# Gates of the dense stage computed for two keys at a time, and looser order edges on the row steps

## The chip, the core and the metric

One NeuronCore of a Trainium2 chip runs the whole program in one launch. The metric is device time in microseconds (us). TensorE (PE) does matmuls and weight loads (PEld), VectorE (DVE) and ScalarE (ACT) do elementwise work, GpSimd (POOL) issues the indirect row fetches, and SyncE (SP) issues most plain DMAs. Each engine takes its instructions strictly in the order of its own queue.

## What is computed

A residual block on 1024 tokens of width 1024: a mixer (gated delta rule and a linear recurrence), cross attention into 256 memory tokens, and a retrieval layer that picks 128 of 16384 single-neuron experts for each token. The change touches the last of these:

```python
idx = e1 * PEER_NKEYS + e2                # 8 heads x 16 experts for each token
gate = jax.nn.softmax(best, axis=-1)
act = jax.nn.gelu(jnp.einsum('phkd,pd->phk', u_tab[ib], tb)) * gb
out = jnp.einsum('phk,phkd->pd', act, v_tab[ib])
```

All of it is float32.

## The kernel before

The retrieval layer is done in two ways. For tokens 256 to 767 (TD = 512) it is **dense**: all 16384 experts are run through the PE in 128 chunks of 128 experts ("keys" here), with a gate matrix that is zero for experts not chosen. For the other 512 tokens, in four blocks of 128, it is done by **rows**: for each of the 128 chosen experts of a token POOL fetches one row of u (and later of v) for all 128 tokens of the block by an indirect DMA of 512 KB, and DVE does one 128x1024 operation on it, a "row step". That makes 4 blocks x 2 phases x 128 = 1024 row steps.

*The front part* (up to about 1790 us) holds the mixer, the attention, the choice of experts and the gate matrix, interleaved as streams by a function `together` (L1180 on), which chooses the next piece by times that the builder estimates for itself. Row steps are mixed in by `Paced.tick`: each time the estimated PE time since the last one passes `pe.pace`, one `step()` is traced (L1142). In the front part it is also held back while the estimated DVE time is far ahead or the next row isn't estimated to have landed (`late_row`, L1139).

*The dense part* (`dense`, L1020 to L1103) goes through the keys with `hidden(j)` and `out(j)`. `hidden(j)` splits u and v of a key into a high and a low part (ACT makes `uh`, `vh`, DVE `ul`, `vl`), does 24 matmuls of 512 columns into the one PSUM bank `dh`, then ACT applies GELU into `dg`, DVE multiplies by the gates `G[:, :, j % EC]` (a read with a step of 8 elements), ACT casts to `dah`, and DVE makes the low part `dal`. `out(j)` does 24 matmuls for each key in six banks `po`, and, at odd keys, the fourth token block for two keys in a single bank `po3` (12 more matmuls, in two lots of 6), which DVE adds into `acc`. So the PE has 24 + 18 matmuls for an even key and 24 + 30 for an odd one. The order traced is hidden(0), and then for each j: hidden(j+1), out(j). In the dense part the pace is 2250 ns of estimated PE time for a step (`PACE_D`).

A row goes through six buffers (NROW): five fetches are kept ahead, and POOL can issue the next fetch only when the DVE step that used its buffer is over. The framework's scheduler orders each engine's queue after tracing. It takes work by the traced order among what it believes ready, so that an instruction may be put ahead of an earlier one that it believes is still waiting. `tc.keep_in_program_order` gives a row step an edge behind the DVE instruction that was traced directly before it; the scheduler may put it later, but not earlier.

Of the kernel before, what the change touches and what calls it, by code (L numbers as in the profile page):

```python
# [8 lines left out]
F = mybir.dt.float32  # L9
BF = mybir.dt.bfloat16  # L10
FR = mybir.dt.float32r
I32 = mybir.dt.int32
U32 = mybir.dt.uint32
AF = mybir.ActivationFunctionType
OP = mybir.AluOpType
# [3 lines left out]
S = 1024  # L19
# [4 lines left out]
TD = 2 * T  # L24
EC = 8
# [11 lines left out]
HOP, SLACK, WAIT = 100.0, 8000.0, 1000.0  # L37
SHARE = (6.0, 1.0, 6.0, 1.0)
L_NORM, L_STEP, L_CONV, L_SOFT, L_GATE = 14000.0, 2500.0, 4000.0, 6000.0, 1500.0
PACES = (2800.0, 2800.0, 2800.0, 3500.0)  # L40
PACE_G, PACE_D = 3500.0, 2250.0
FIRST = 0
EARLY = T
UNITS = ((0, 1), (128, 1), (256, 2), (512, 2), (768, 2))
# [5 lines left out]
def block_kernel(ctx: ExitStack, tc: tile.TileContext, a):  # L50
# [17 lines left out]
    def moved(n):  # L68
        dma[0] = max(dma[0], pe.at) + n / 360.0
        return dma[0] + 2000.0  # L70

    class Engine:

        def __init__(self, engine, fixed, rate):
            self.engine, self.fixed, self.rate = engine, fixed, rate
            self.at = self.total = self.end = 0.0

        def __getattr__(self, op):
            call = getattr(self.engine, op)

            def f(*args, **kw):
                r = call(*args, **kw)  # L82
                aps = [x for x in list(args) + list(kw.values()) if isinstance(x, bass.AP)]
                if op == "dma_start":
                    moved(prod(args[0].shape) * 4)
                else:
                    self.spend(aps)
                return r
            return f

# [32 lines left out]
    pe = Paced()  # L123
    sp = Engine(nc.sync, 0.0, 0.0)
    act, dve = Engine(nc.scalar, 200.0, 0.72), Engine(nc.vector, 68.0, 1.04)
# [119 lines left out]
    def c8(t):  # L245
        return t.rearrange("p (c m) -> p c m", c=8)
# [67 lines left out]
    def mm3(out, l, r, start, stop):  # L314
        pe.matmul(out, l[0], r[0], start=start, stop=False)
        pe.matmul(out, l[0], r[1], start=False, stop=False)
        pe.matmul(out, l[1], r[0], start=False, stop=stop)
# [692 lines left out]
    def u_raw(p, j):  # L1010
        raw = p.tile([128, D], F, name="ur", bufs=2)
        sp.dma_start(raw, a["ut"][j])
        return raw

    def v_raw(p, j):
        raw = p.tile([128, D], F, name="vr", bufs=2)
        sp.dma_start(raw, a["v"][j * 128:(j + 1) * 128, :])
        return raw

    def dense(p1, p, ps, hT, raws):  # L1020
        hhi, hlo = hT
        NT = TD // 128
        res = [[ps.tile([128, 512], F, name=f"po{t}{d}") for d in range(2)] for t in range(NT - 1)]
        acc = p.tile([128, D], F, name="acc", bufs=1)
        row3 = D0 + TD - 128
        sp.dma_start(acc, x2d[row3:row3 + 128, :])

        def split(raw, name, bufs):
            hi = p1.tile([128, D], FR, name=name + "h", bufs=bufs)
            lo = p1.tile([128, D], FR, name=name + "l", bufs=bufs)  # L1030
            act.copy(hi, raw)
            dve.tensor_sub(lo, raw, hi.bitcast(F))
            return hi, lo

        G = [None]
        A, V = {}, {}

        def hidden(j):
            if j % EC == 0:
                G[0] = p.tile([128, TD, EC], F, name="G", bufs=2)  # L1040
                sp.dma_start(G[0], gd[j // EC])
            u, v = raws.pop(0) if raws else (u_raw(p1, j), v_raw(p1, j))
            uh, ul = [c8(t) for t in split(u, "u", 2)]
            V[j] = split(v, "v", 3)
            h = ps.tile([128, TD], F, name="dh")
            for c in range(8):
                mm3(h, (uh[:, c, :], ul[:, c, :]), (hhi[:, c, :], hlo[:, c, :]), c == 0, c == 7)
            g = p.tile([128, TD], F, name="dg", bufs=2)
            act.activation(g, h, AF.Gelu_apprx_tanh)
            dve.tensor_mul(g, g, G[0][:, :, j % EC])  # L1050
            ah = p.tile([128, TD], FR, name="dah", bufs=3)
            al = p.tile([128, TD], FR, name="dal", bufs=3)
            act.copy(ah, g)
            dve.tensor_sub(al, g, ah.bitcast(F))
            A[j] = (ah, al)

        xs = []

        def add_res(t):
            x = xs[0][:, t, :]  # L1060
            for d in range(2):
                ds = slice(d * 512, (d + 1) * 512)
                dve.tensor_add(x[:, ds], x[:, ds], res[t][d])
            finish(x, D0 + t * 128, xs[0][:, NT - 1, :])

        def out(j):
            def part(o, i, t, d, start, stop):
                ts, ds = slice(t * 128, (t + 1) * 128), slice(d * 512, (d + 1) * 512)
                mm3(o, [x[:, ts] for x in A[i]], [x[:, ds] for x in V[i]], start, stop)

            def last(d):
                o = ps.tile([128, 512], F, name="po3")
                for i in (j - 1, j):
                    part(o, i, NT - 1, d, i < j, i == j)
                ds = slice(d * 512, (d + 1) * 512)
                dve.tensor_add(acc[:, ds], acc[:, ds], o)

            if j == 124:
                xs.append(p.tile([128, TD, EC], F, name="G", bufs=2).rearrange("p (t d) k -> p t (d k)", t=4))
                sp.dma_start(xs[0][:, 0:NT - 1, :],  # L1080
                             x2d[D0:row3, :].rearrange("(t p) m -> p t m", p=128))
            if j % 2:
                last(0)
            for t in range(NT - 1):
                for d in range(2):
                    part(res[t][d], j, t, d, j == 0, j == 127)
                if j == 127:
                    add_res(t)
            if j % 2:
                last(1)  # L1090
                for i in (j - 1, j):
                    A.pop(i), V.pop(i)

        hidden(0)
        for j in range(128):
            if j + 1 < 128:
                hidden(j + 1)
            for _ in range(LATE):
                next(late[0], None)
            out(j)  # L1100
        finish(acc, row3, xs[0][:, NT - 1, :])
# [1 line left out]

    todo, fetched = [], []
    blocks = {}

    def add_block(row, rs, idx, gt):
# [29 lines left out]
    def late_row():  # L1139
        return bool(fetched) and fetched[0][4] > max(dve.at, pe.at) + WAIT  # L1140

    def step():  # L1142
        while todo and len(fetched) < NROW - 1:
            fetch()
        if not fetched:
            return False
        row, ph, k, t, _ = fetched.pop(0)
        B = blocks[row]
        if ph == "u":
            if k == 0:  # L1150
                dve.scalar_tensor_tensor(B["h"], B["h"], B["rs"], B["w"], op0=OP.mult, op1=OP.mult)
                B["hd"] = gat.tile([128, 128], F, name="hdot", bufs=1)
            tc.keep_in_program_order(
                dve.scalar_tensor_tensor(t, t, 1.0, B["h"], op0=OP.mult, op1=OP.mult,
                                         accum_out=B["hd"][:, k:k + 1]))
            if k == 120:
                B["x"] = row_of(NROW + 1)
                sp.dma_start(B["x"], x2d[row:row + 128, :])
            if k == 127:
                B["a"] = gat.tile([128, 128], F, name="ga", bufs=1)  # L1160
                act.activation(B["a"], B["hd"], AF.Gelu_apprx_tanh)
                dve.tensor_mul(B["a"], B["a"], B["gt"].rearrange("p h k -> p (h k)"))
        else:
            tc.keep_in_program_order(
                dve.scalar_tensor_tensor(B["x"], t, B["a"][:, k:k + 1], B["x"], op0=OP.mult, op1=OP.add))
            if k == 127:
                finish(B["x"], row, t)
        return True
# [74 lines left out]
    def attended():  # L1243
        yield from memory(att, KT, VM)
        first.rank = FIRST
        for t0, nb in UNITS:
            while t0 not in done:
                yield None
            yield from attend(att, t0, nb, KT, VM)
        while D0 + TD - T not in begun:  # L1250
            yield None
        front.close()
        d1 = ctx.enter_context(tc.tile_pool(name="duv", bufs=1))
        dn.append(d1)
        raws.extend((u_raw(d1, j), v_raw(d1, j)) for j in range(2))

    dn, hT, raws, begun = [], [], [], set()
    wp = front.enter_context(tc.tile_pool(name="wp", bufs=1))
    att = front.enter_context(tc.tile_pool(name="att", bufs=1))
    KT = att.tile([128, 8, MEM], F, name="KT")  # L1260
# [3 lines left out]
    fps.close()  # L1264
    with tc.tile_pool(name="dn", bufs=1, side="right") as d2, \
            tc.tile_pool(name="dps", bufs=1, space=bass.MemoryType.PSUM) as dps:
        pe.pace, pe.real = PACE_D, False
        dense(dn[0], d2, dps, hT, raws)
    while step():
        pass  # L1270

# [63 lines left out]
```

## Time and profile before

| quantity | us |
|---|---|
| median of 3 runs | 3276.9 (3274.99 to 3279.72) |
| time of the profiled execution | 3275.43 |
| span of the profiled execution, first to last instruction | 3273.7 |
| PE busy in the span | 2987.4 (91%) |
| DVE busy | 2737.6 (84%) |
| ACT busy | 1277.8 (39%) |
| POOL busy | 1431.4 (44%) |

The busy shares are means over two unlike parts, so they are read by stretch below: the front part up to 1790 us, the dense part after it, and in the front part the stretches with and without row steps.

### The profile page before, as it was taken

To read this page: it belongs to the slowest core of one execution; us is meant where nothing else is said; L and a number is where in the kernel's file an instruction comes from. 1 tells how busy PE (TensorE), PEld (TensorE's weight loads), DVE (VectorE), ACT (ScalarE), POOL (GpSimd) and SP (SyncE) were. 2 spreads that over 40 slices of the span, in tenths; PEclk is the share of its full clock that TensorE was granted. 3 is DMA by queue.
4 is the path that set the end of the run, shared out by engine and by line. 5 is a ranking of instruction groups with operands and counts; after the bars stand their busy time and mean duration, and the time that the engine had idled before them with its cause. 6 is when DMAs were issued, how large, how long until landed. Compare 5 with 4: busy or idle time off the path is not lost.

```text
span 3273.7 us, 46519 instructions
## 1 busy us (share of the span) xinstructions
PE 2987.4 (91%) x16212; PEld 2559.6 (78%) x16212; DVE 2737.6 (84%) x5999; ACT 1277.8 (39%) x2694; POOL 1431.4 (44%) x1046
## 2 busy tenths in 40 slices
PE   6999997699999989898857899999999999999998
PEld 6888887678988878887746677888888878888886
DVE  7634776877787898898999798888999989899998
ACT  6843363236322642376357332222222222222222
POOL 0000233334433344243345375556666655566663
PEclk9999998899999999998968899999999999999999
DMA  5346788688888769888888799999999899999995
GB/s 170 110 143 208 248 281 308 232 285 284 308 292 291 251 223 332 301 281 302 303 289 273 267 329 334 333 340 330 344 333 328 319 334 333 330 341 327 339 331 198
DMA packets 321547, 941.66 MB, mean 288 GB/s; under 512 B 28912, under 2 KB 108832, under 8 KB 319264
## 3 DMA queue, kind: packets, MB, share of 16 engines
q0 software_dynamic: 148048, 538.04, 46.8%
q1 hardware_dynamic: 107216, 367.08, 30.9%
q10 hardware_dynamic: 66048, 33.56, 3.7%
q8 instruction: 128, 2.10, 0.3%
q14 instruction: 107, 0.88, 0.1%
HBM read 894.53 MB, written 44.04 MB: 287 GB/s over the span
## 4 chain that ended last, share of the span: by engine, by line
PE 61%; DVE 20%; DMA 9%; ACT 5%; issue 3%; POOL 1%; SPq 0%; ACTq 0%; DVEq 0%; POOLq 0%
PE dh L106 21%; PE po L106 20%; PE pj L106 15%; DVE rb L82 6%; DMA rb<-in_u,idx 4%; PE gd L106 3%; DVE oh L82 3%; DMA gd<-stage 2%; DMA w<-in_pwq 1%; PE tp L111 1%; PE sc L106 1%; DVE cy L82 1%; ACT ohg L82 1%; DVE i L82 1%; ACT L82 1%
## 5 line engine op out<-in xcount | busy, mean ns | idle before, releaser
L1134 POOL DMA_INDIRECT rb<-in_u,idx x512 | 677.4, 1323 | 1111.9 <-DVE rb L82 497.0
L1134 POOL DMA_INDIRECT rb<-in_v,idx x512 | 745.0, 1455 | 690.3 <-DVE rb L82 478.7
L82 DVE SCALAR_TENSOR_TENSOR rb<-rb 128x1024 f32<-128x1024 f32 x512 | 613.1, 1218 | 90.2 <-DMA rb<-in_u,idx 90.2
L82 DVE SCALAR_TENSOR_TENSOR rb<-rb,ga 128x1024 f32<-128x1024 f32 x512 | 655.0, 1279 | 11.2 <-DMA rb<-in_v,idx 4.9
L106 PE MATMUL pj<-hT,w 128*128 128x256 f32 (+1 forms) x2880 | 590.6, 358 | 16.2 <-DMA w<-in_pwq 11.8
L106 PEld LDWEIGHTS pj<-hT,w 128*128 128x128 f32 x2880 | 491.8, 195 | 73.5 <-DMA w<-in_pwq 13.1
L106 PE MATMUL dh<-hT_h,uh 128*128 128x512 f32 x1024 | 407.1, 398 | 21.4 <-ACT dg L82 20.7
L106 PE MATMUL po<-vh,dah 128*128 128x512 f32 x1024 | 404.8, 395 | 9.7 <-DVE acc L82 8.7
L106 PE MATMUL dh<-hT_l,uh 128*128 128x512 f32 x1024 | 406.2, 397 | 0.0
L106 PE MATMUL dh<-hT_h,ul 128*128 128x512 f32 x1024 | 406.1, 397 | 0.0
L106 PE MATMUL po<-vh,dal 128*128 128x512 f32 x1024 | 405.2, 396 | 0.4 <-DVE dal L82 0.4
L106 PE MATMUL po<-vl,dah 128*128 128x512 f32 x1024 | 405.3, 396 | 0.0
L82 ACT CAST uh<-ur 128x1024 fp32r<-128x1024 f32 x128 | 134.7, 1052 | 561.0 <-PE dh L106 352.8
L106 PE MATMUL gd<-ohg,oh 128*128 128x128 f32 x1024 | 183.7, 332 | 81.4 <-ACT ohg L82 54.5
L106 PEld LDWEIGHTS dh<-hT_h,uh 128*128 128x128 f32 x1024 | 193.2, 189 | 69.3 <-ACT dg L82 21.6
L106 PEld LDWEIGHTS gd<-ohg,oh 128*128 128x128 f32 x1024 | 163.8, 228 | 101.9 <-ACT ohg L82 80.5
L106 PEld LDWEIGHTS po<-vh,dah 128*128 128x128 f32 x1024 | 192.3, 188 | 58.4 <-DVE acc L82 10.0
L106 PEld LDWEIGHTS dh<-hT_h,ul 128*128 128x128 f32 x1024 | 193.0, 189 | 47.0
L106 PEld LDWEIGHTS dh<-hT_l,uh 128*128 128x128 f32 x1024 | 193.2, 189 | 46.4
L106 PEld LDWEIGHTS po<-vl,dah 128*128 128x128 f32 x1024 | 192.3, 188 | 47.2
L106 PEld LDWEIGHTS po<-vh,dal 128*128 128x128 f32 x1024 | 192.3, 188 | 47.1 <-DVE dal L82 0.8
L82 DVE TENSOR_TENSOR ul<-ur,uh 128x1024 fp32r<-128x1024 f32 x128 | 156.0, 1222 | 48.7 <-ACT uh L82 27.6
(339 smaller groups left out, 4757.4 us busy)
## 6 DMA issues: line engine op xcount, KB each, us to landing
ur<-in_ut SPq DMA_DIRECT2D x128, 512.0 KB
vr<-in_v SPq DMA_DIRECT2D x128, 512.0 KB
w<-in_wA SPq DMA_DIRECT2D x80, 512.0 KB
w<-in_pwq SPq DMA_DIRECT2D x80, 512.0 KB
gd<-stage ACTq DMA_DIRECT2D x32, 1024.0 KB
G<-gd SPq DMA_DIRECT2D x16, 2048.0 KB
w<-in_wout SPq DMA_DIRECT2D x40, 512.0 KB
w<-in_wq SPq DMA_DIRECT2D x40, 512.0 KB
```

The costliest lines, as they stand in the source:

```text
L82: r = call(*args, **kw)
L106: self.engine.matmul(out, l, r, **kw)
L111: self.engine.transpose(out, i, ident)
L1134: pool.indirect_dma_start(out=t, out_offset=None, in_=a[ph], in_offset=bass.IndirectOffsetOnAxis(ap=B["idx"][:, k:k + 1], axis=0))
```

## The change

Three things are done.

1. In `dense`, the GELU of keys 2i and 2i+1 is written side by side into one tile `dg` of 128 x 512 x 2; after the odd key one DVE multiplication, one ACT cast and one DVE subtraction of 128x1024 serve both keys, in place of two of each of 128x512. `dah` and `dal` have two buffers of two keys each in place of three of one. The split of v moves out of `hidden` into `values`. The order traced becomes hidden(0), values(0), hidden(1), and then for each j: values(j+1), hidden(j+2), out(j).
2. `behind` replaces `keep_in_program_order`: a row step gets an edge behind the last DVE instruction that the builder estimates to end no later than 1000 ns after the step's row lands (also an estimate of the builder), and one behind the row step before it.
3. The pace in the dense part is worked out so that all steps that are left fit in 1316000 ns of estimated PE time.

```diff
-PACE_G, PACE_D = 3500.0, 2250.0
+PACE_G, DENSE = 3500.0, 1316000.0
...
+                    self.log.append((r.ins, self.at))
...
         def hidden(j):
...
-            u, v = raws.pop(0) if raws else (u_raw(p1, j), v_raw(p1, j))
+            u = raws.pop(0) if raws else u_raw(p1, j)
             uh, ul = [c8(t) for t in split(u, "u", 2)]
-            V[j] = split(v, "v", 3)
...
-            g = p.tile([128, TD], F, name="dg", bufs=2)
-            act.activation(g, h, AF.Gelu_apprx_tanh)
-            dve.tensor_mul(g, g, G[0][:, :, j % EC])
-            ah = p.tile([128, TD], FR, name="dah", bufs=3)
-            al = p.tile([128, TD], FR, name="dal", bufs=3)
-            act.copy(ah, g)
-            dve.tensor_sub(al, g, ah.bitcast(F))
-            A[j] = (ah, al)
+            if j % 2 == 0:
+                g2[0] = p.tile([128, TD, 2], F, name="dg", bufs=2)
+            g = g2[0]
+            act.activation(g[:, :, j % 2], h, AF.Gelu_apprx_tanh)
+            if j % 2:
+                dve.tensor_mul(g, g, G[0][:, :, j % EC - 1:j % EC + 1])
+                ah = p.tile([128, 2, TD], FR, name="dah", bufs=2)
+                al = p.tile([128, 2, TD], FR, name="dal", bufs=2)
+                g = g.rearrange("p t k -> p k t")
+                act.copy(ah, g)
+                dve.tensor_sub(al, g, ah.bitcast(F))
+                for k in range(2):
+                    A[j - 1 + k] = (ah[:, k, :], al[:, k, :])
+
+        def values(j):
+            V[j] = split(rawv.pop(0) if rawv else v_raw(p1, j), "v", 3)
...
         hidden(0)
+        values(0)
+        hidden(1)
         for j in range(128):
             if j + 1 < 128:
-                hidden(j + 1)
+                values(j + 1)
+            if j + 2 < 128:
+                hidden(j + 2)
...
+    def behind(r, land):
+        past = [i for i, t in dve.log[:-1] if t <= land + WAIT][-1:] + steps[-1:]
+        for i in past:
+            tc.add_manual_dep(r.ins, i.name, mybir.DependencyInfo(
+                mybir.DependencyClass.NoSync, mybir.DependencyReason.DATA), reason="rows")
+        steps.append(r.ins)
+        del dve.log[:-200]
...
-            tc.keep_in_program_order(
-                dve.scalar_tensor_tensor(t, t, 1.0, B["h"], op0=OP.mult, op1=OP.mult,
-                                         accum_out=B["hd"][:, k:k + 1]))
+            behind(dve.scalar_tensor_tensor(t, t, 1.0, B["h"], op0=OP.mult, op1=OP.mult,
+                                            accum_out=B["hd"][:, k:k + 1]), land)
...
-        pe.pace, pe.real = PACE_D, False
-        dense(dn[0], d2, dps, hT, raws)
+        pe.pace, pe.real = DENSE / (2.0 * (S - TD) - stepped[0]), False
+        dense(dn[0], d2, dps, hT, raws, rawv)
```

The v row steps get `behind` in the same way, and the two u and v loads that are issued ahead go into two lists in place of one.

## Rows read from the trace of the kernel before

**Rows 1.** Busy time by stretch: us, then PE, PEld, DVE, ACT, POOL, PEclk, DMA share, GB/s
```profile
430.00:1400.00 970.00, 866.82 (x5538) 784.49 (x5537) 783.22 (x2384) 391.90 (x957) 359.56 (x309) 0.95 0.80 280
1400.00:1790.00 390.00, 304.33 (x1727) 270.23 (x1726) 360.06 (x1082) 245.69 (x682) 155.10 (x118) 0.86 0.88 292
1835.00:3255.00 1420.00, 1409.99 (x6032) 1132.64 (x6031) 1293.78 (x1535) 403.95 (x513) 871.58 (x567) 1.00 0.90 325
```
**Rows 2.** Chain that ended last, two keys of the dense part: start, us, what
```profile
2042.57 7.00 PE po L106 x30
2049.56 5.60 PE dh L106 x24
2055.17 4.20 PE po L106 x18
2059.36 5.60 PE dh L106 x24
```
**Rows 3.** ACT in order of time, first GELU of the dense part: start, us
```profile
1811.67 1.28 ACT L82 ACT_TABLE_LOAD   x1 [15.07 <-DMA gd<-stage]
```
**Rows 4.** PE's waits from 1780 us on: us in total, times, longest
```profile
PE dh L106 <- ACT dg L82: 20.7, 2, 17.9
PE po L106 <- DVE acc L82: 8.7, 3, 5.2
```
**Rows 5.** Groups of DVE, 2030 to 2595 us: busy us, mean ns, idle before
```profile
L82 DVE SCALAR_TENSOR_TENSOR rb<-rb,ga 128x1024 f32<-128x1024 f32 x118 | 151.2, 1282 | 2.2
L82 DVE SCALAR_TENSOR_TENSOR rb<-rb 128x1024 f32<-128x1024 f32 x114 | 136.6, 1220 | 19.8 <-DMA rb<-in_u,idx 19.8
...
L82 DVE TENSOR_TENSOR ul<-ur,uh 128x1024 fp32r<-128x1024 f32 x51 | 62.2, 1223 | 18.4 <-ACT uh L82 10.2 <-PE po L106 8.0
L82 DVE TENSOR_TENSOR dg<-dg,G 128x512 f32<-128x512 f32 x51 | 61.1, 1197 | 0.0
...
L82 DVE TENSOR_TENSOR dal<-dg,dah 128x512 fp32r<-128x512 f32 x50 | 34.5, 691 | 9.7 <-ACT dah L82 8.9
```
**Rows 6.** Groups of ACT from 1780 us on, same columns
```profile
L82 ACT CAST dah<-dg 128x512 fp32r<-128x512 f32 x128 | 79.4, 621 | 289.5 <-DVE dg L82 289.5
L82 ACT ACTIVATE dg<-dh 128x512 f32<-128x512 f32 x128 | 75.4, 589 | 6.0 <-PE dh L106 5.9
```
**Rows 7.** DVE in order of time at the fourth block's first u rows
```profile
2630.11 1.23 DVE L82 SCALAR_TENSOR_TENSOR rb<-rb 128x1024 f32<-128x1024 f32 x1 [5.68 <-DMA rb<-in_u,idx]
...
2635.02 0.68 DVE L82 TENSOR_TENSOR acc<-acc,po 128x512 f32<-128x512 f32 x1
```
**Rows 8.** PE in order of time, just behind rows 7
```profile
2635.76 0.79 PE L106 MATMUL po<-vh,dah 128*128 128x512 f32 x1 [5.19 <-DVE acc L82]
```
**Rows 9.** PE's waits, 430 to 1790 us: total, times, longest
```profile
PE gd L106 <- ACT ohg L82: 54.5, 51, 5.3
PE gd L106 <- DVE oh L82: 15.5, 5, 6.2
...
PE sc L106 <- DVE i L82: 0.2, 1, 0.2
```
**Rows 10.** DVE's waits, 430 to 1790 us
```profile
DVE rb L82 <- DMA rb<-in_u,idx: 34.0, 18, 4.2
DVE X L82 <- PE pj L106: 33.0, 18, 7.1
```
**Rows 11.** Groups of DVE up to 1790 us: busy us, mean ns, idle before
```profile
L82 DVE SCALAR_TENSOR_TENSOR rb<-rb 128x1024 f32<-128x1024 f32 x256 | 306.9, 1216 | 41.1 <-DMA rb<-in_u,idx 41.1
L82 DVE SCALAR_TENSOR_TENSOR rb<-rb,ga 128x1024 f32<-128x1024 f32 x188 | 239.6, 1274 | 4.7 <-DMA rb<-in_v,idx 3.6
```
**Rows 12.** DVE in order of time, a hole in the front part
```profile
1025.81 0.17 DVE L82 TENSOR_TENSOR xg<-ab,dtb 128x8 f32<-128x8 f32 x1 [6.47 <-ACT ab L82]
...
1026.13 1.28 DVE L82 SCALAR_TENSOR_TENSOR rb<-rb,ga 128x1024 f32<-128x1024 f32 x1
```
**Rows 13.** Instructions on the row buffers from 1780 us: ns min/median/max, first and last start
```profile
L82 DVE SCALAR_TENSOR_TENSOR rb<-rb,ga x330: 1266/1284/1346, 1779.5 to 3246.8; 128x1024 f32<-128x1024 f32 x165
```

## The prediction: what the change does to the time

> **What bounds the kernel now.** I read the busy time by stretch first, then the chain that ended last, then the PE's waits in the two parts, and last the DVE rows behind those waits.
>
> In the dense part the PE is busy 1409.99 of 1420.00 us at full clock, so it is idle for 10.0 us; DVE is busy 91% and the DMA engines 90% [rows 1]. The chain shows why: two keys take 7.00 + 5.60 + 4.20 + 5.60 = 22.40 us of nothing but matmuls [rows 2], 96 of them at 233 ns, and 64 such pairs are 1433.6 us. The change touches no matmul, so this floor stays. Above it lie the start, where the PE waits twice for the GELU, 20.7 us in all with 17.9 in one piece [rows 4], and those 10.0 us, of which 8.7 are waits for the `acc` addition on DVE [rows 4].
>
> In the front part the limit changes hands. From 430 to 1790 us, where row steps run, the PE is busy 866.82 + 304.33 of 1360 us, so it is idle for 189 us; DVE is busy 81% up to 1400 us and 92% after that [rows 1]. The PE's waits put 77.8 us on DVE: 21 rows, from 15.5 us for `oh` down to 0.2 us for `i`; 54.5 us go to ACT's `ohg` [rows 9], which is made from DVE's `oh`. Here, and only here, can the change move tens of us.
>
> **Part 1, gates for two keys.** Removed for a pair: two multiplications of 1197 ns and two subtractions of 691 ns on DVE, 3.78 us [rows 5], and two casts of 621 ns on ACT [rows 6]. Added: one subtraction of 128x1024, which I put at 1223 ns from `ul`, of the same size and operation [rows 5], one cast, and one multiplication of 128x1024 that reads the gates as pairs of neighbours with a step of 8 elements between pairs. The trace has no such read. Its bounds are 1.22 us, a contiguous operation of that size, and 2 x 1197 = 2.39 us, if each element costs what it costs now [rows 5]. Today's multiplication takes 506 ns more than the subtraction of the same shape, so it is the step of the read that costs. I take 1.5 us, nearer the lower end, since half of the jumps are gone. DVE then does 2.7 us for a pair where it did 3.78, a relief of 1.1 us (bounds 0.16 and 1.33) in 22.4 us: its busy share falls from 91% to 86%.
>
> The Trainium skill ("SBUF — State Buffer", Specifications) says that the memory has 16-byte lines and that an operand reads at full rate when at least two accesses fall in a line. By that the paired read is a full-rate one, the multiplication takes the lower bound and the relief is 1.33 us; the dense term below would stay near 4 us, and with the upper bound it would be about 1. The 506 ns above agree that a read with one element in a line is slow; no row here shows two.
>
> What does it buy? DVE isn't what the PE waits for in the steady state, so nearly all of it lies in cover. It can shorten only the 10.0 us. Of these, 5.19 us are one wait [rows 8]: DVE had stood 5.68 us for a u row that had not landed, and then had two `ul`, one `dg` and one `acc` to do before the PE could go on [rows 7]. A faster `dg` helps there by about 1 us; whether the row step stands in front of `ul` at all is a matter of part 2. I take **4 us** of the 10.0 (bounds 0 and 10.0).
>
> What it costs: the gates of an even key now wait for the odd key's. After `dh` of the odd key the chain is GELU 0.59, multiplication up to 2.39, cast 1.05 at most by `uh`'s size (I take 2 x 0.621 = 1.24), subtraction 1.22, 5.4 us in all [rows 5, 6]. The new order puts `out` of the odd key before (7.00) and the next `hidden` (5.60) between, 12.6 us [rows 2]; 7 us are left, five row steps of 1.28 [rows 5]. Nothing on the PE is queued behind it sooner, so I cost it at nothing; without that cover each us beyond 12.6 would cost 64 us. The values' split stays one key ahead, the single bank `dh` is still released by a GELU that runs under `out`, and SP now issues u two keys ahead and v one, with two buffers for each as now: nothing.
>
> The first wait stays. ACT stood 15.07 us until the last gate transfer `gd<-stage` had landed [rows 3]; the gate multiplication needs that same data, and the change moves neither.
>
> **Part 2, looser edges.** A row step could not go before the DVE instruction traced just ahead of it, even if its row lay there and that instruction was waiting for the PE. Now it can, down to the point at which its row is estimated to have landed, a few steps earlier at most, since six buffers hold what is fetched. The trace has such a hole: DVE stood idle for 6.47 us for `xg`, and the row step followed right behind [rows 12]. DVE has 187 us of idle time from 430 to 1400 us [rows 1], 33.0 of it ahead of `X` alone [rows 10]. Steps that fill such holes are not in the way afterwards. Up to 1790 us the steps take 306.9 + 239.6 = 546.5 us [rows 11], 48% of the DVE time from 430 us on (783.22 + 360.06 us). If they have that share in the 77.8 us, 37 us of PE waiting could be theirs. That is the upper bound. Against it, a step put too early holds DVE, and all that is queued behind it (`X`, `oh`, `W`, then the PE), until the row lands: DVE stood 34.0 us for u rows in 18 waits [rows 10], and if that doubles and passes on to the PE in full it costs 34 us. I take a gain of a third of 37, **12 us**, because the fetch of a row is released by the step six before it: if all steps move forward, so do the fetches, and the time for landing between them stays.
>
> **Part 3, the pace.** 444 of the 1024 steps ran before 1790 us [rows 11]; 1316000 / 580 is 2269 ns for a step in place of 2250. The last step, which began at 3246.8 [rows 13], would come up to 12 us later by that, and earlier by what part 2 lets it move. Between 0 and +6 us in the tail; I take 0.
>
> **Sum.** 3273.7 - 4 - 12 = 3257.7 us of span. The profiled execution took 3275.43, and the median of the runs is 3276.9, so I forecast 3276.9 - 16 = **3261 us**, 0.5% less. What this measurement can tell from no change is about 0.2%, so "same" runs from 3270 to 3283.
>
> **The rivals.**
> *Holes filled well.* All of the 37 us, and most of the 10.0: 3276.9 - 45 = 3232. For it: 92% busy DVE just before 1790 us, and `ohg`, which lies behind `oh`. Against it: many of the 21 waits are chains with no step in them.
> *Hidden anyway.* DVE's relief lies under the matmuls, the scheduler finds the same order or trades one wait for another: 3276.9 - 4 = 3273. This also covers the case that the paired multiplication takes 2.39 us and the change shares nothing.
> *Rows taken too early* (the other side). The builder's estimate of a landing is earlier than the landing, the scheduler fills holes with steps whose rows are still under way, and DVE stands with the PE's next operand behind it. Where this happens today it passes on nearly in full: 5.68 us on DVE, 5.19 on the PE [rows 7, 8]. If the 34.0 us double and half passes on, with the dense gain lost, it is 3276.9 + 17 = 3294; in full, 3311. It decides as soon as the added waits for rows that reach the PE exceed what the filled holes give, some 16 us.
> *The pair is late.* If row steps in a bunch push the 5.4 us chain past 12.6 by 0.3 us on average, it costs 64 x 0.3 = 19 us: 3296.
>
> **Chances.** Forecast (3247 to 3270) 0.42, holes filled well 0.15, hidden anyway 0.18, rows too early 0.20, late pair 0.05. So faster 0.57, same 0.18, slower 0.25. The range reaches from 3225, a little under the good case, to 3298, a little over the two slow ones at half size.
>
> **What would show it.** Right: the group `dg<-dg,G` with 64 operations of 128x1024 at 1.2 to 1.6 us; the pair in the chain still 22.40 us; the PE's first wait of some 18 us still there; DVE-released PE waits from 430 to 1790 us falling from 77.8 to about 65, and the dense part starting some 12 us before 1790. Wrong: DVE's waits for `rb<-in_u` or `rb<-in_v` well over 34.0 in the front part; a repeated wait of `po` for `dal`; a dense part that starts later than 1790 us, which would be enough to lose the forecast, since the dense part alone can give no more than 10 us.

## The result, and the profile after

| quantity | before | after |
|---|---|---|
| median of 4 runs each, us | 3278.31 (3274.99 to 3283.97) | 3239.35 (3233.96 to 3248.56) |
| ratio after/before, 95% interval | | 0.9883 (0.9865 to 0.9901) |
| profiled execution: time, span | 3275.43, 3273.7 | 3242.79, 3241.0 |
| dense part begins (first `dh` matmul) | 1789.87 | 1766.27 |
| PE's first waits of the dense part (`dh` for `dg`) | 20.7 | 11.3 |
| PE's waits of `po` for `acc` | 8.7 | 7.2 |

The kernel became 39 us faster, 1.2%. The forecast was 16 us: right in sign, too small by more than half. In the spans 32.7 us are gone: 23.6 ahead of the dense part, 9.4 in its first waits, 1.5 in the waits for `acc`; the tail behind the last `po` matmul, 13.1 us before, is 14.9.

The kernel after has one line number more for DVE and ACT (L83) and two more for matmuls (L108). Its busy time by stretch (us, then PE, PEld, DVE, ACT, POOL, PEclk, DMA share, GB/s) answers to [rows 1]:

```profile
430.00:1400.00 970.00, 869.05 (x5594) 784.33 (x5593) 791.54 (x2453) 402.26 (x982) 377.29 (x318) 0.95 0.82 288
1400.00:1790.00 390.00, 296.31 (x1692) 262.56 (x1690) 350.84 (x1028) 243.08 (x659) 158.32 (x113) 0.88 0.88 293
1835.00:3225.00 1390.00, 1382.80 (x5911) 1111.00 (x5910) 1190.96 (x1388) 393.16 (x441) 778.22 (x553) 1.00 0.89 325
```

In the dense part DVE is now busy 1190.96 of 1390 us, 86%, where it was 91%. The chain that ended last, in order of time, is what it was in [rows 2], 22.40 us for two keys:

```profile
2054.27 5.60 PE dh L108 x24
2059.87 7.00 PE po L108 x30
```

(`out` does 18 matmuls for each key in the six banks, 4.20 us, and 12 more at an odd key; the 24 that the section on the kernel before gives for the six banks are too many.)

The PE's waits from 1755 us on (total, times, longest) answer to [rows 4], ACT's first GELU of the dense part to [rows 3]; there is no wait of `po` for `dal`:

```profile
PE dh L108 <- ACT dg L83: 11.3, 2, 8.5
PE po L108 <- DVE acc L83: 7.2, 4, 3.3
```
```profile
1766.24 0.37 ACTq L83 DMA_DIRECT2D gd<-stage  x1
...
1779.92 0.62 ACT L83 ACTIVATE dg<-dh 128x512 f32<-128x512 f32 x1 [10.86 <-DMA gd<-stage]
```

The last gate transfer takes 13.7 us from its issue to the GELU behind it; before it was issued at 1789.85 and ended ACT's wait at 1811.67, 21.8 us.

The groups of DVE from 2030 to 2595 us and of ACT from 1755 us on (busy us, mean ns, idle before) answer to [rows 5, 6]:

```profile
L83 DVE TENSOR_TENSOR ul<-ur,uh 128x1024 fp32r<-128x1024 f32 x50 | 61.1, 1222 | 60.5 <-ACT uh L83 46.8 <-issue 8.8 <-PE dh L108 4.7
L83 DVE TENSOR_TENSOR dg<-dg,G 128x1024 f32<-128x1024 f32 x25 | 30.6, 1224 | 0.0
L83 DVE TENSOR_TENSOR dal<-dg,dah 128x1024 fp32r<-128x1024 f32 x25 | 30.5, 1219 | 2.9 <-ACT dah L83 2.9
```
```profile
L83 ACT ACTIVATE dg<-dh 128x512 f32<-128x512 f32 x128 | 81.0, 633 | 24.5 <-PE dh L108 13.7 <-DMA gd<-stage 10.9
L83 ACT CAST dah<-dg 128x1024 fp32r<-128x1024 f32 x64 | 72.4, 1131 | 130.7 <-DVE dg L83 130.7
```

The paired multiplication costs what a contiguous one of that size does (1224 against 1222 ns for `ul`), so a pair takes 2.44 us on DVE and the relief is 1.33 us, the upper bound. That is what the Trainium skill ("SBUF — State Buffer", Specifications) gives by its 16-byte lines: two fp32 neighbours fall in one line. ACT pays a little: GELU takes 633 ns in place of 589, and the cast 1131 ns where the prediction put 1.05 us at most and took 1.24.

Last, DVE's waits in the front part. Before, row steps stood 34.0 us for u rows in 18 waits [rows 10]. After:

```profile
DVE X L83 <- PE pj L108: 43.3, 22, 4.0
...
DVE rb L83 <- DMA rb<-in_u,idx: 5.7, 7, 2.0
```

Nearly all of that wait is gone, and the prediction has no reason for it: it reckoned that these 34.0 us could only grow.

The PE's waits up to the dense part moved from one engine to another. Those for DVE fell from 77.8 to 59.1 us; those for ACT rose from 86.2 to 101.4. The two lines that grew most, before (430 to 1790 us, beside `ohg` in [rows 9]) and after (430 to 1766 us):

```profile
PE tp L111 <- ACT oT L82: 6.1, 3, 4.4
```
```profile
PE gd L108 <- ACT ohg L83: 62.0, 47, 8.7
PE tp L113 <- ACT oT L83: 24.9, 8, 10.5
```

So the PE's idle time from 430 us to the dense part hardly changed: 188.8 us before, 184.2 after.

### The profile page after: what moved, and what is told of

It reads as the page before. It is cut to its first block, busy times and chain, and to the rows that moved or that the text cites. A ratio compares the mean times of both kernels' runs of the same rounds, so it can differ in the third digit from the quotient of the medians.

```text
span 3241.0 us, 46225 instructions
## 1 busy us (share of the span) xinstructions
PE 2973.1 (92%) x16212; PEld 2546.1 (79%) x16212; DVE 2647.0 (82%) x5871; ACT 1277.0 (39%) x2627; POOL 1371.7 (42%) x1046
## 4 chain that ended last, share of the span: by engine, by line
PE 61%; DVE 22%; DMA 8%; ACT 6%; issue 3%; POOL 0%; SPq 0%; ACTq 0%; DVEq 0%; POOLq 0%
PE dh L108 21%; PE po L108 20%; PE pj L108 15%; DVE rb L83 7%; DVE oh L83 3%; PE gd L108 3%; DMA gd<-stage 2%; PE tp L113 2%; DVE i L83 1%; PE sc L108 1%; DMA w<-in_pwq 1%; DVE s L83 1%; DVE mr L83 1%; ACT L83 1%; DMA w<-in_wA 1%
## 5 line engine op out<-in xcount | busy, mean ns | idle before, releaser
L1149 POOL DMA_INDIRECT rb<-in_u,idx x512 | 670.6, 1310 | 1114.7 <-DVE rb L83 459.4
L1149 POOL DMA_INDIRECT rb<-in_v,idx x512 | 692.1, 1352 | 709.7 <-DVE rb L83 512.4
L83 DVE SCALAR_TENSOR_TENSOR rb<-rb,ga 128x1024 f32<-128x1024 f32 x512 | 655.6, 1281 | 14.4 <-DMA rb<-in_v,idx 8.6
L83 DVE SCALAR_TENSOR_TENSOR rb<-rb 128x1024 f32<-128x1024 f32 x512 | 611.9, 1216 | 41.8 <-DMA rb<-in_u,idx 39.2
L108 PE MATMUL pj<-hT,w 128*128 128x256 f32 (+1 forms) x2880 | 588.1, 357 | 15.7 <-DMA w<-in_pwq 10.3
L108 PEld LDWEIGHTS pj<-hT,w 128*128 128x128 f32 x2880 | 490.6, 194 | 73.1 <-DMA w<-in_pwq 12.2
L83 ACT CAST uh<-ur 128x1024 fp32r<-128x1024 f32 x128 | 134.5, 1051 | 730.9 <-PE dh L108 634.4
L108 PE MATMUL dh<-hT_h,uh 128*128 128x512 f32 x1024 | 407.7, 398 | 12.0 <-ACT dg L83 11.3
L108 PE MATMUL po<-vh,dah 128*128 128x512 f32 x1024 | 404.8, 395 | 7.2 <-DVE acc L83 7.2
L108 PE MATMUL dh<-hT_l,uh 128*128 128x512 f32 x1024 | 406.8, 397 | 0.0
L108 PE MATMUL dh<-hT_h,ul 128*128 128x512 f32 x1024 | 406.5, 397 | 0.0
L108 PE MATMUL po<-vl,dah 128*128 128x512 f32 x1024 | 405.4, 396 | 0.0
L108 PE MATMUL po<-vh,dal 128*128 128x512 f32 x1024 | 405.3, 396 | 0.0
L83 DVE TENSOR_TENSOR ul<-ur,uh 128x1024 fp32r<-128x1024 f32 x128 | 156.1, 1221 | 147.2 <-ACT uh L83 106.5
L108 PE MATMUL gd<-ohg,oh 128*128 128x128 f32 x1024 | 179.7, 329 | 78.2 <-ACT ohg L83 62.0
L108 PEld LDWEIGHTS dh<-hT_h,uh 128*128 128x128 f32 x1024 | 193.7, 189 | 60.1 <-ACT dg L83 12.2
L108 PEld LDWEIGHTS gd<-ohg,oh 128*128 128x128 f32 x1024 | 160.9, 225 | 97.6 <-ACT ohg L83 88.3
L108 PEld LDWEIGHTS po<-vh,dah 128*128 128x128 f32 x1024 | 192.2, 188 | 55.9 <-DVE acc L83 9.0
L108 PEld LDWEIGHTS dh<-hT_h,ul 128*128 128x128 f32 x1024 | 193.5, 189 | 47.1
L108 PEld LDWEIGHTS dh<-hT_l,uh 128*128 128x128 f32 x1024 | 193.7, 189 | 46.6
L108 PEld LDWEIGHTS po<-vl,dah 128*128 128x128 f32 x1024 | 192.3, 188 | 47.2
L108 PEld LDWEIGHTS po<-vh,dal 128*128 128x128 f32 x1024 | 192.4, 188 | 46.3
```

What stands on the lines that cost most here:

```text
L108: self.engine.matmul(out, l, r, **kw)
L1149: pool.indirect_dma_start(out=t, out_offset=None, in_=a[ph], in_offset=bass.IndirectOffsetOnAxis(ap=B["idx"][:, k:k + 1], axis=0))
```

## Experiments

The change puts *two* edges on a row step: the **first edge**, behind the last DVE work estimated to be over when the row lands (it replaces an edge behind the instruction traced just before, so it is looser), and the **second edge**, behind the row step before it (`steps[-1:]`). The prediction weighed only the first. The theories: (A) the looser first edge fills holes, as predicted; (B) the second edge is what counts, because without it row steps pass one another; (C) the dense stage by pairs brings the gain, by DVE's relief or by its order.

What (B) says can be seen in the order in which DVE's queue stands. The fetches take eight semaphores in turn, DMASW0 to DMASW7, in the order in which POOL issues them (all 1024 do, in the traces). So a run of u steps should wait for them in turn. Four neighbouring u steps of the third block in the queue of the kernel before, and of f1 (below), which adds the second edge and nothing else; the rows were traced in the order of their numbers:

```
before  u step of row 28 [waits DMASW7_49]     f1  u step of row 26 [waits DMASW6_49]
        u step of row 29 [waits DMASW1_49]         u step of row 27 [waits DMASW7_49]
        u step of row 26 [waits DMASW4_49]         u step of row 28 [waits DMASW0_49]
        u step of row 27 [waits DMASW0_49]         u step of row 29 [waits DMASW1_49]
```

A v step adds into `B["x"]`, so the data keep v steps in order. A u step writes a column of its own, and nothing holds two of them together but the edge to the DVE instruction traced between them: the scheduler may put each later, one more than the other. Where a step asks for a row fetched after others that lie there already, DVE stands, the buffers of the waiting rows stay taken, and POOL fetches nothing.

**One part at a time.** e1 has both edges with the old dense stage, e2 the pairs with the old edge, both at the old pace; e3 is the kernel after at the old pace; e4 the kernel after with the old edge in the dense part alone.

```diff
 e1, from before (both kinds of step):
-            tc.keep_in_program_order(
-                dve.scalar_tensor_tensor(t, t, 1.0, B["h"], op0=OP.mult, op1=OP.mult,
-                                         accum_out=B["hd"][:, k:k + 1]))
+            behind(dve.scalar_tensor_tensor(t, t, 1.0, B["h"], op0=OP.mult, op1=OP.mult,
+                                            accum_out=B["hd"][:, k:k + 1]), land)
 e2, from after:
     def behind(r, land):
-        past = [i for i, t in dve.log[:-1] if t <= land + WAIT][-1:] + steps[-1:]
...
+        tc.keep_in_program_order(r)
 e2 and e3, from after:
-        pe.pace, pe.real = DENSE / (2.0 * (S - TD) - stepped[0]), False
+        pe.pace, pe.real = 2250.0, False
 e4, from after:
     def behind(r, land):
+        if not pe.real:
+            tc.keep_in_program_order(r)
+            return
```

> The looser edges alone, with the dense part and the pace of the kernel before. Holes theory (steps go into the idle time of DVE and are out of the way afterwards): the dense part starts as early as in the changed kernel, 1766 us in place of 1790, so 24 us less at that point, and about 3250 us in all, the rest of the gain being the pairs'. Pairs theory (the lighter DVE work of the dense part carries the gain): about 3275, within 0.2% of before.

Measured: 3260.62 us, ratio 0.9946 (0.9925 to 0.9967). The dense part begins at 1776.4 and takes 1470.7 us to the end of its last `po` matmul, as before (1470.7): its first waits fell from 20.7 to 9.8 us, but `po` waits 14.3 us for `acc` in place of 8.7. So both edges alone give 0.5%, all of it ahead of the dense part.

> The pairs alone: every row step pinned behind the DVE instruction traced before it, pace 2250. Holes theory: the dense part starts at 1790 us as before, and the lighter DVE work gives no more than the 10 us of PE idle time after 1835 us: 3266 to 3275. Pairs theory: 3245 or less. If the first wait of the dense part falls from 17.9 to about 8.5 us here, it is the order of the dense part that shortens it; if it stays near 18, it is the edges.

Measured: 3377.89 us, ratio 1.0303 (1.0273 to 1.0333). The pairs alone make the kernel 3% *slower*, though they take work off DVE; neither theory of the expectation had that. DVE's and PE's waits of e2 in the dense part (total, times, longest):

```profile
DVE rb L83 <- DMA rb<-in_u,idx: 194.9, 105, 7.6
```
```profile
PE po L108 <- DVE acc L83: 77.6, 24, 9.4
PE dh L108 <- ACT dg L83: 15.8, 2, 12.9
```

One wait in order of time, on DVE, on POOL and on the PE:

```profile
2020.00 1.22 DVE L83 TENSOR_TENSOR ul<-ur,uh 128x1024 fp32r<-128x1024 f32 x1
2028.82 1.22 DVE L83 SCALAR_TENSOR_TENSOR rb<-rb 128x1024 f32<-128x1024 f32 x1 [7.61 <-DMA rb<-in_u,idx]
...
2031.25 1.22 DVE L83 TENSOR_TENSOR ul<-ur,uh 128x1024 fp32r<-128x1024 f32 x1
2032.39 1.22 DVE L83 TENSOR_TENSOR dg<-dg,G 128x1024 f32<-128x1024 f32 x1
2033.52 0.68 DVE L83 TENSOR_TENSOR acc<-acc,po 128x512 f32<-128x512 f32 x1
```
```profile
2023.57 0.94 POOL L1149 DMA_INDIRECT rb<-in_u,idx  x1 [0.30 <-issue]
2030.32 1.81 POOL L1149 DMA_INDIRECT rb<-in_u,idx  x1 [5.82 <-DVE rb L83]
```
```profile
2034.26 0.79 PE L108 MATMUL po<-vh,dah 128*128 128x512 f32 x1 [5.42 <-DVE acc L83]
```

The landings in the trace show that the step stood out of turn. The row that it waited for had the semaphore DMASW5 and landed at 2028.80; the three rows fetched just before it (DMASW2, 3 and 4) had landed at 2019.57, 2024.43 and 2027.04, and their steps ran only from 2034 us on. The busy share of e2's DMA engines over the 30 us from 2005 to 2035 (one digit for 0.75 us) shows the cost to the transfers: three zeros, from 2030.5 to 2032.75, when the rows fetched so far have been moved and the next fetch, which POOL could not issue before 2030.32, is not yet under way:

```profile
DMA  9985779879998999878979989999999994000998
```

> The changed kernel with the pace of before, 2250 ns a step. By the sum of the prediction the pace is worth between 0 and 6 us, and nothing is the likeliest: 3237 to 3242. If the steps that end later are what lengthens the tail, this one is 2 to 5 us shorter than the changed kernel.

Measured: 3243.91 us, ratio 0.99 (0.9879 to 0.9921); the kernel after, run again (g4, below), has 0.9893 (0.9876 to 0.9911). The pace is worth nothing that can be measured.

> The changed kernel with the looser edges up to the dense part only; in the dense part each step is pinned behind the DVE instruction traced before it. Holes theory: front part as in the changed kernel (dense part from 1766 us), total within 5 us of it, 3235 to 3245, since in the dense part DVE is not what the PE waits for. If the edges inside the dense part matter, the waits of po for acc and of dh for the GELU go back to some 9 and 20 us and the total to about 3252.

Measured: 3359.35 us, ratio 1.0232 (1.0199 to 1.0266). The dense part begins at 1770.0, as in the kernel after, and is then 113 us longer than there (1572.6 against 1459.9 us), with 209.9 us of waits for u rows and 88.6 for `acc`. That is far more than its expectation allowed in either case. The pairs need the edges of the dense part.

**Which of the two edges?** f1 and f2 keep the old first edge and add the second, on the old dense stage and on the pairs; f3 and f4 have the looser first edge without the second, on the pairs and on the old dense stage; g1 has the second alone.

```diff
 f1 (old dense stage and pace), f2 (after), in behind:
-        past = [i for i, t in dve.log[:-1] if t <= land + WAIT][-1:] + steps[-1:]
-        for i in past:
+        tc.keep_in_program_order(r)
+        for i in steps[-1:]:
 f3 (from after), f4 (from e1):
-        past = [i for i, t in dve.log[:-1] if t <= land + WAIT][-1:] + steps[-1:]
+        past = [i for i, t in dve.log[:-1] if t <= land + WAIT][-1:]
 g1 (from after):
-        past = [i for i, t in dve.log[:-1] if t <= land + WAIT][-1:] + steps[-1:]
+        past = steps[-1:]
```

> The kernel before with one edge more for each row step: besides the edge behind the DVE instruction traced before it, one behind the row step before it. Row order theory (in the kernel before, u steps run out of the order in which their rows are fetched, so DVE waits for a late row while an earlier one lies there; it is the second edge of the change that mends it): DVE's waits for u rows from 430 to 1790 us fall from 34.0 to about 6, and the total is about 3260, as with both edges (e1_edges, 3260.6). Holes theory (it is the looser first edge that gains): no change, about 3275.

Measured: 3256.7 us, ratio 0.9939 (0.9913 to 0.9965). One edge more on the kernel before is worth as much as both edges of the change (e1, 0.9946). DVE's waits for u rows in the front part fall from 34.0 to 13.4 us (about 6 were expected):

```profile
DVE rb L83 <- DMA rb<-in_u,idx: 13.4, 10, 3.0
```

> The changed kernel with the tight first edge (behind the DVE instruction traced before the step) and the second edge (behind the row step before). Row order theory: about as fast as the changed kernel, 3235 to 3255, against 3378 for the pairs without the second edge (e2_pairs). Holes theory: it stays slow, over 3340, since the steps of a pair still stand pinned behind its DVE work.

Measured: 3248.94 us, ratio 0.9914 (0.9882 to 0.9946). Against e2, which is 3% slower than before and differs only by this edge and the pace, it is 129 us less.

> The changed kernel with the looser first edge alone; the edge behind the row step before is left out. Row order theory: slow like e2_pairs, over 3340, with DVE waiting some 200 us for u rows from 1790 us on. Holes theory: as the changed kernel, 3235 to 3250.

Measured: 3303.75 us, ratio 1.0076 (1.0047 to 1.0105). This lies between the two theories of the expectation: slower than before, but less than expected without the second edge, with 129.6 us of waits for u rows in the dense part where some 200 were expected.

> The dense part and pace of the kernel before, with the looser first edge alone and no edge behind the row step before. Row order theory: no gain over before, 3270 or more, since u steps run out of row order at least as often. Holes theory: about 3260, as e1_edges.

Measured: 3350.31 us, ratio 1.0231 (1.02 to 1.0262). The edge that the prediction took for the whole of part 2 makes the old dense stage 2.3% slower by itself, and DVE's waits for u rows in the front part are as long as before:

```profile
DVE rb L83 <- DMA rb<-in_u,idx: 37.6, 19, 6.1
```

With the pairs (f3) it is 0.8% slower than the kernel before, though 2.2% faster than the pairs with the old edge (e2, at the old pace). So without the second edge the time goes either way, by several per cent. With it the kind of first edge makes no difference that can be measured: 0.9939 and 0.9946 on the old dense stage (f1, e1), 0.9914 and 0.9883 or 0.9893 with the pairs (f2, the kernel after, g4), all with overlapping intervals.

> The changed kernel with the edge behind the row step before alone: nothing holds a row step back until its row is estimated to have landed. Rows too early (the slow rival of the prediction): DVE's waits for rows from 430 to 1790 us double against before, from 34.0 to 70 us or more, and the total is 17 to 34 us over the changed kernel: 3256 to 3275. If the order of the rows is all that matters, within 6 us of it: 3234 to 3246.

Measured: 3353.82 us, ratio 1.0224 (1.0199 to 1.0249). Steps in order, but free to come as early as the scheduler likes. By 1200 us 390 of them have begun, where the kernel after has 279. The front part of g1, busy time by stretch as above, and its waits on DVE up to the dense part:

```profile
430.00:1400.00 970.00, 799.07 (x5004) 716.90 (x5005) 858.53 (x2317) 366.73 (x861) 520.94 (x437) 0.92 0.91 338
```
```profile
DVE rb L83 <- DMA rb<-in_u,idx: 37.7, 40, 2.4
DVE rb L83 <- DMA rb<-in_v,idx: 27.0, 30, 2.9
```

The PE has 799.07 us of work in that stretch in place of 869.05; its waits put on DVE up to the dense part come to 114.8 us (59.1 after), and the dense part begins at 1824.1. Hardly any of these waits is out of turn: in 0.9 of the 37.7 us another u row lay there. This is the rival "rows taken too early", and a first edge, the looser one or the old one (f1, f2), is what keeps a kernel from it.

The next table shows where the order is lost. For each u step of the dense part that waits for a row by itself (some have no such wait), it counts those that ask for the fetch two places, or three and more, behind the one of the step's own place in DVE's queue. Beside it stand the profiled execution's waits; "out of turn" is the time of DVE's waits for u rows in which at least one other u row, not yet used, had landed (by the landings in the trace).

| kernel | second edge | 2 late | 3 or more late | DVE for u rows, us | of it out of turn | `po` for `acc`, us | first `dh` to last `po`, us |
|---|---|---|---|---|---|---|---|
| before | no | 62 | 2 | 49.1 | 48.8 | 8.7 | 1470.7 |
| f3 | no | 30 | 11 | 129.6 | 123.2 | 37.9 | 1506.7 |
| f4 | no | 20 | 38 | 119.3 | 114.8 | 71.0 | 1548.8 |
| e2 | no | 26 | 118 | 194.9 | 190.7 | 77.6 | 1566.9 |
| e4 | not in the dense part | 34 | 117 | 209.9 | 207.5 | 88.6 | 1572.6 |
| f1 | yes | 2 | 0 | 13.7 | 6.3 | 9.8 | 1469.3 |
| after | yes | 2 | 0 | 32.3 | 6.7 | 7.2 | 1459.9 |

Without the second edge nearly all of DVE's waiting for u rows is out of turn. In the front part it is 28.4 of the 34.0 us before and all of the 37.6 us in f4, but 3.0 of 13.4 in f1 and none of the 5.7 after. The kernels with more steps that ask for a row three or more places on have the longer dense parts (e2 and e4 are nearly alike in both). Before had nearly as many steps out of place (194 of 254; e2 213 of 234), but most of them by one or two places, and that cost little. It was the same freedom; which order the scheduler finds in it depends on all the rest of DVE's work, and nothing in the kernel holds it to the harmless one.

**Where the dense part starts.** The same runs sort by edge, all in us from the profiled executions. "Running" is the start plus the PE's first waits for `dg`; "last gates" is the time from the issue of the last `gd<-stage` to the GELU it holds back (1.3 us of it is a table load where one lies between); "fetches" are POOL's row issues in that time.

| first edge | second | kernels | dense begins | running | last gates | fetches | PE idle from 430 us to the dense part |
|---|---|---|---|---|---|---|---|
| old | no | before, e2 | 1789.9, 1797.2 | 1810.6, 1813.0 | 23.1, 18.1 | 9, 6 | 188.8, 188.9 |
| looser | no | f4, f3 | 1776.6, 1786.2 | 1787.3, 1794.5 | 13.2, 13.0 | 3, 2 | 186.5, 188.4 |
| old | yes | f1, f2 | 1770.6, 1769.0 | 1787.8, 1783.5 | 19.6, 16.8 | 9, 6 | 175.6, 177.1 |
| looser | yes | after, e1, e3, e4, g2, g4 | 1766.3 to 1776.4 | 1775.4 to 1786.2 | 7.8 to 15.5 | 2 to 4 | 184.2 to 189.2 |
| none | yes | g1 | 1824.1 | 1827.6 | 11.3 | 0 | 226.2 |

With the looser edge alone the matmuls run some 21 us sooner (means 1791 against 1812): 12 us of it are in the start and 9 in the first wait. The second edge gives 26 us (1786 against 1812), 24 of them in the start. They don't add: both together give 30. These are means of few executions, and executions of one front program differ by up to 10 us (f3 and f4), so the differences among the rows that have a new edge are not settled. The 12 us are also not the predicted ones, though the number is the same: the prediction had them from the PE's waits, and with the looser edge the PE is idle as long as before.

The first wait goes with the row fetches in the time in which the last gates are written: 9 or 6 with the old edge, 2 to 4 with the looser one. A longer stretch also has room for more fetches, and no run changes the fetches alone, so which of the two drives the other is argued and not shown.

The transfers beside the last gates, of the kernel before (1789.8 to 1811.7 us) and after (1766.2 to 1779.9): queue and kind, then packets, MB, share of 16 engines. q0 holds the rows.

```profile
q0 software_dynamic: 1701, 6.18, 73.1%
q10 hardware_dynamic: 2100, 1.06, 16.3%
```
```profile
q0 software_dynamic: 812, 2.93, 56.6%
q10 hardware_dynamic: 2217, 1.12, 27.7%
```

Beside the same 1 MB of gates twice as many bytes of rows had to go, with the DMA engines nearly full in both (0.95 and 0.94 of their time).

**What do the pairs do, once the order is kept?** g2 is the kernel after with the gates key by key and everything else kept (the order of keys too); g3 gives key 1's hidden layer a free bank, so that it needn't wait for key 0's GELU; g4 is the kernel after, unchanged, beside them.

```diff
 g2 (from after), in hidden(j):
+            g = p.tile([128, TD], F, name="dg", bufs=2)
+            act.activation(g, h, AF.Gelu_apprx_tanh)
+            dve.tensor_mul(g, g, G[0][:, :, j % EC])
+            ah = p.tile([128, TD], FR, name="dah", bufs=4)
+            al = p.tile([128, TD], FR, name="dal", bufs=4)
...
 g3 (from after):
-            h = ps.tile([128, TD], F, name="dh")
+            h = ps.tile([128, TD], F, name="po3" if j == 1 else "dh")
```

> The changed kernel with the gates key by key: hidden still runs two keys ahead, but the gate multiplication, the cast and the subtraction are done for each key by itself, so DVE gets its 1.3 us a pair back. If the lighter DVE work is what the pairs give (the two kernels with and without them, e1_edges and the changed one, are some 20 us apart), the total is about 3255 to 3262. If it is the order (hidden two keys ahead gives the gates more time), about 3240.

Measured: 3250.11 us, ratio 0.9898 (0.9876 to 0.9919).

> The changed kernel once more, beside the three others of this call: 3234 to 3248.

Measured: 3246.3 us, ratio 0.9893 (0.9876 to 0.9911). No difference from g2: the 1.33 us of DVE work for a pair, 85 us in all, are worth nothing that can be measured. What is left of the step from e1 (0.9946) to g2 (0.9898) is the order, `hidden` two keys ahead of `out` and the values' split on its own, with the new pace (worth nothing, e3) and one more buffer for `dah` and `dal`; in e1 `po` waits 14.3 us for `acc`, in g2 8.4. These two ratios put it at some 16 us. From f1 to f2, where both keep the old first edge, it is 8 us with overlapping intervals, so its size is not settled.

> The changed kernel with the hidden layer of key 1 in the bank po3, which is free until out(1). The PE can then do 24 matmuls more (5.6 us) while ACT waits for the last gate transfer, and the second wait of 2.8 us goes too. If the wait at the start of the dense part is on the path, 6 to 9 us less than the changed kernel run beside it: about 3232. If the start has another limit (the gates have to land anyway before out(0)), no change.

Measured: 3241.03 us, ratio 0.9884 (0.9865 to 0.9903). The PE's first waits in g3 (from 1750 us on):

```profile
PE dh L108 <- ACT uh L83: 4.1, 1, 4.1
...
PE dh L108 <- ACT dg L83: 0.7, 1, 0.7
```

In g4 they are 9.8 us. The 5 us are gained in the trace and agree with the medians (3241.03 against 3246.3), but the intervals overlap.

## Why the prediction was right in sign and too small

**Right.** The floor of 22.40 us for two keys stayed. The pair is not late: no wait of `po` for `dal`. The pace is worth nothing (e3). PE waits put on DVE from 430 us to the dense part fell from 77.8 to 59.1 us, forecast 65.

**Mis-sized.** The paired multiplication took its lower bound, 1.224 us, where 1.5 was taken. It didn't matter, as g2 shows: this relief lies in cover.

**The step that failed is part 2, the term of 12 us.** It describes the change as one edge, a looser one, and prices it as a third of the PE's waits that row steps might cause. Both the edge and the path were wrong.

*The edge.* The gain that stays needs the second edge, which the prediction names in no sum: alone on the kernel before it gives 0.6% (f1). The looser edge alone loses (f4, 2.3% slower), and beside the second it adds nothing that can be measured. The reason is in [rows 10]: the 34.0 us were taken for rows that come late, a limit of the fetch. They were mostly (28.4 us) steps that stood for a row out of turn: the looser edge alone leaves them (37.6 us in f4), the second alone makes them 13.4 (f1), both 5.7, with the same rows and the same six buffers. The 5.68 us of [rows 7] were such a wait too: the row was fetched at 2618.00 and landed at 2630.09, while that of the fetch just before it had landed at 2622.52, and its step ran only at 2637.61.

*The path.* The waits for DVE fell as forecast, but those for ACT rose by 15.2 us, so the PE's idle time ahead of the dense part fell by 4.6 us only. That the dense part starts 23.6 us earlier, where 12 were forecast, is right in direction and mostly for another reason, as said under "Open".

**"The first wait stays" failed too.** The argument was that the gate multiplication needs the same data and that the change moves neither. But the transfer holds the GELU itself, which reads no gates: ACT's idle time in [rows 3] and the 10.86 us after lie ahead of it, and the first multiplication of the kernel before runs only at 1822.8, 10 us behind that GELU. And the traffic beside the transfer moved: 9 or 6 fetches with the old edge, 2 to 4 with the looser one, and the PE's first waits fall from 20.7 to 11.3 us. The dense part gave 10.8 us in all, 9.4 of them here and only 1.5 in the waits for `acc`, where the prediction put its 4.

**The rivals.** "Rows taken too early" has the right mechanism and too small a price: it was put at 17 to 34 us, and g1, in which it happens, loses 74. Waits for rows alone are 64.7 us there up to the dense part; besides, steps done early take DVE's time from the work that the PE needs next, so that its waits for DVE are 114.8 us where they were 77.8. "Hidden anyway" holds for DVE's relief. No rival had the case of e2, the dense stage by pairs alone at +3%: the order of DVE's queue changes with any change to its work, and where it is held together by one neighbour only it can come out much worse. No rival had the gain of the second edge either; that the forecast's direction came true with part 2 wrong is luck.

**Open.** Of the 23.6 us ahead of the dense part the PE's idle time accounts for 4.6 (188.8 us from 430 us on before, 184.2 after); its busy time fell by 19.0 us, 1171.03 to 1152.06, spread over nearly all groups of matmuls. Most of that is the clock. Of this busy time 143.8 us before and 116.2 after lie where the granted clock was at the lower of its two levels, 1.2 of 2.4 GHz; 27.6 us less at half speed are worth 13.8 of the 19.0. Counted from the span's start to the dense part, the busy time is 1531 to 1555 us in the fourteen traces; weighted by the granted clock it is 1460 to 1466 us in thirteen and 1474 in g1. What made the clock fall less, fewer stops or chance, no run tells apart: the kernel after, run again as g4, has 134.2 us at the lower level and begins its dense part at 1774.0. Nor does any run show how much of the step from f1 to the kernel after is the order of the dense stage and how much the looser edge.

## What to carry to other kernels

Where instructions are chained only to their neighbour in the traced order, look whether they can pass one another, and whether each takes from a queue that is served in turn; one edge from each to the one before it keeps the order, and cost nothing here; something must still hold them back until their data are near (g1). A wait for a transfer is first to be asked whether it stands for the next one in the queue or for a later one. And read every edge that a change adds: here a stage rewritten to relieve an engine was worth nothing by that relief, and an edge in passing decided between 3% slower (e2) and 1% faster (f2).

## What the runs showed of the hardware that was not expected

A fp32 read of two neighbours with a step of 8 elements between pairs runs at the contiguous rate on DVE (1224 ns against 1222 for 128x1024), where single elements at that step took 1197 ns for half as many [rows 5]. A GELU that writes every second element cost ACT 633 ns in place of 589 [rows 6]. A 1 MB transfer of gates took 13.7 us from its issue to the end of the wait for it with 2.93 MB of row fetches beside it, and 21.8 us with 6.18 MB.
